# Where norms, state attention and output weights stand in a streaming encoder step on one Trainium2 core

## The chip, the core and the metric

The kernel is one launch on one NeuronCore of a Trainium2 chip. The metric is device time in microseconds, the median of repeated executions, lower is better. TensorE (PE) does the matrix products, VectorE (DVE) and ScalarE (ACT) the elementwise work, GpSimd (POOL) broadcasts and issues part of the DMAs, and SyncE (SP) issues the rest.

## What is computed

One layer of a hybrid encoder over 2048 prompt tokens and 8 x 16 sample tokens, model width 1024, all in float32. Cut to what matters:

```python
u = rms_norm(x, norm_mix) @ w_in             # 21 tiles of 128 columns, split among four mixers
mix = concat(ssd(u), swa(u), shortconv(u), conformer(u))
x = x + mix @ w_out
hf = rms_norm(x, norm_ffn)
x = x + (silu(hf @ w_gate) * (hf @ w_up)) @ w_down      # d_ff = 2816 = 22 tiles
y = rms_norm(x, norm_final)
```

The sample tokens carry their own history: `ssd` starts from a state `h0`, `swa` (attention) also reads a cache of 128 keys and values for each of 8 sequences. The state after the step is an output too.

## The kernel before, in words

Features lie on the partitions, tokens on the free axis. The tokens are cut into five chunks c0 to c4 of 256, 512, 512, 512 (384 of the prompt and the 128 sample tokens) and 384. A float32 product is made as three products of rounded operands: each weight tile (128 x 1024) and each activation tile is split in a high part (a copy on ACT) and a low part (a subtraction on DVE), and `group` (L239 to L241) issues high x high, high x low and low x high. A *unit* is one weight tile against one chunk: 8 slices x 3 matmuls = 24 matmuls into one PSUM bank of the four of pool `pm`.

`load_w` either loads a raw weight tile of 512 KB into one of two `fr` buffers and splits it into one of three `w` buffers (L204 on ACT, L184 on DVE), or, where an earlier chunk has stored the split pair in DRAM (`kept`, 1 MB, stored from the POOL queue, L227), loads that pair straight into `w` (L219). `keep(c, n)` stores the even tiles at c1 and the rest at c2. `proj_out` asked for that as well, so that the tiles of `w_out` were loaded raw by c0, by c1 and, for four of them, by c2, and split by four loads at c2, eight at c3 and eight at c4.

`weave(units, (tokens, a, b), ...)` sets the order. It runs the units one after the other and spreads each list of side tokens evenly over the unit numbers a to b; a token is one step of a generator up to its next `yield`. Matmuls of a token come behind the last matmul of the unit before it (`issue_after`). The program is then put in one order for each engine when it is built: an instruction stands where its buffers and inputs are expected to be ready, earlier text goes first, and weight loads are pulled ahead (`high_priority`). On the chip each engine and each DMA queue works its list strictly in that order.

The pieces that matter here:

- `norm1` (L334) makes the eight normalised, split input tiles `xn` of a chunk, `norm2` (L866) those of the feed-forward part, `final` (L931) the output. Each begins by spreading a row of 1/rms over the partitions with a few matmuls (L272), and then goes through eight tiles. `norm1` reads its tiles again from DRAM into `nt`, of which there are three buffers that `add_square` also uses for the squares of `proj_out`.
- `proj_out` (L840) loads the residual tile `x2[m]` (L849), adds the PSUM bank to it (L184) and then squares it. There are eight `x2` buffers. The one of unit m is free when `final` of the chunk before has written tile m to DRAM (L939).
- `raw_tiles` gives one of two `raw` buffers to the outputs `a`, `h`, `B`, `C`, `x0`, `x1` of `proj_in`. With the sample chunk c3, the history is loaded into it and the new history stored from it (L398, 12 KB) before it is free again. The buffer of `a0` stays in use until the 31 taps of the conformer convolution are done.
- `mixers` makes the tokens of a chunk: three (two, four) blocks of prompt attention and ssd, the sample's attention and ssd where there is a sample, the conformer convolution, and the ends. `attend_sample` and `load_h0` put the state, keys and values into `act` buffers, of which there are 16; at c3 eight hold `xn` of c3 and eight the feed-forward input of c2 until the last `proj_in` unit of c3 (`z1`) has read them.

The last 896 tokens (c3, c4) go through the feed-forward part together at the end, as two halves of 448 (`quad`, `product`); `drain` adds and squares the result and `final2` norms and stores it.

Of the kernel before, what the change touches and what calls it, by code (L numbers as in the profile page):

```python
# [17 lines left out]
P = 128  # L18
# [100 lines left out]
def stream_step(ctx: ExitStack, tc: tile.TileContext, cfg, x, w_in, w_out, w_gu, w_down, tab, con, dist_p, dist_s,  # L119
# [23 lines left out]
    def mk(pool_, shape, tag, dt=F32, **kw):  # L143
        uid[0] += 1
        return pool_.tile(shape, dt, tag=tag, name=f"{tag}_{uid[0]}", **kw)
# [188 lines left out]
    def norm1(c):  # L334
        T, o = c["T"], c["off"]
        r = spread(c["r1"], T)
        c["xn"] = []
        for k in range(KT):
            if "x" in c:
                xt = c["x"][k]  # L340
            else:
                xt = mk(np_, [P, TM], "nt", bufs=B["nt"])[:, :T]
                sync.dma_start(xt, x[:, k, o:o + T])
            stt(xt, xt, T_("gmix", k), r, ALU.mult, ALU.mult)
            d = mk(ap, [P, 2, TM], "act", F32R)
            split(d, xt, T)
            c["xn"].append(d)
            if k == 3:
                yield
        yield  # L350

# [436 lines left out]
    def mixers(c, early=False):  # L788

        st = []  # L790
        c["mix"] = [None] * 8

        def add(*gens):

            todo = [[g, n] for g, n in gens]
            while any(n for _, n in todo):
                for t in todo:
                    if t[1]:
                        st.append(t[0])
                        t[1] -= 1  # L800

        if c["Ts"]:
            def load_h0():
                c["h0"] = []
                for i in range(2):
                    c["h0"].append(mk(ap, [P, DEC_B // 2, 256], "act"))
                    pool.dma_start(c["h0"][i], h0[:, 4 * i:4 * i + 4])
            add((once(load_h0), 1))
            add((attend_sample(c), 3), (ssd(c, c["Tp"], True), 2))
        short = once(lambda: [mix_tile(c, 4 + t, c["u"][f"y{t}"][:, :c["T"]]) for t in range(2)])  # L810
        if not early:
            add((short, 1))
        convs = [(j, k, min(31, k + 8)) for j in range(2) for k in range(0, 31, 8)]
        nb = c["nt"]
        for b in range(nb):
            add((attend_prompt(c, b), 3), (ssd(c, b * P, False), 2))
            mine = convs[len(convs) * b // nb:len(convs) * (b + 1) // nb] if not early else []
            for j, k0, k1 in mine:
                add((once(lambda j=j, k0=k0, k1=k1: conf_conv(c, j, k0, k1)), 1))
        if early:  # L820
            c["blocks"] = len(st)
            for j, k0, k1 in convs:
                add((once(lambda j=j, k0=k0, k1=k1: conf_conv(c, j, k0, k1)), 1))
            add((short, 1))
        add((end_conf(c), 3), (end_ssd(c), 3))
        add((once(lambda: [mix_tile(c, 2 + g, c["u"][f"q{g}"][:, :c["T"]]) for g in range(2)]), 1))
        return st
# [12 lines left out]
    def proj_out(c):  # L840
        T, o = c["T"], c["off"]
        c["x2"] = []

        def unit(m):
            if m == 0:
                c["ss"] = mk(np_, [P, TM], "ns", bufs=1)[:, :T]
            park = c["i"] >= cfg.nfirst
            x2 = mk(np_, [P, TM], "nt", bufs=B["nt"]) if park else mk(np_, [P, TM], "x2", bufs=8)
            sync.dma_start(x2[:, :T], x[:, m, o:o + T])  # L849
            wh, wl = load_w(w_out[m], [KT, P], len(W_IN_TILES) + m, keep(c, m))  # L850
            ps = mk(pm, [P, 512], "pm")
            group(ps, T, [(wh[:, k], wl[:, k], c["mix"][k]) for k in (4, 5, 2, 3, 0, 1, 6, 7)])
            tt(x2[:, :T], x2[:, :T], ps[:, :T], ALU.add)
            if park:
                pool.dma_start(mid[:, m, o - tail_off:o - tail_off + T], x2[:, :T])
            add_square(c["ss"], x2[:, :T], T, m == 0)
            c["x2"].append(x2)

        return [lambda m=m: unit(m) for m in range(KT)]
# [6 lines left out]
    def norm2(c):  # L866
        T = c["T"]
        r = rstd_of(c["ss"], T, D)
        yield
        r = spread(r, T)  # L870
        c["hf"] = []
        for k in range(KT):
            t = mk(np_, [P, TM], "nt", bufs=B["nt"])[:, :T]
            stt(t, c["x2"][k][:, :T], T_("gffn", k), r, ALU.mult, ALU.mult)
            d = mk(ap, [P, 2, TM], "act", F32R)
            split(d, t, T)
            c["hf"].append(d)
        yield

    def ffn(c):  # L880
# [50 lines left out]
    def final(c):  # L931
        T, o = c["T"], c["off"]
        r = rstd_of(c["ss"], T, D)
        yield
        r = spread(r, T)
        for k in range(KT):
            t = c["x2"][k][:, :T]
            stt(t, t, T_("gfin", k), r, ALU.mult, ALU.mult)
            (sync if c["i"] == last else pool).dma_start(y[:, k, o:o + T], t)  # L939
        yield  # L940


# [31 lines left out]
                j += 1  # L974
        return out

    for t in twice(norm1_stats(chunks[0])) + twice(norm1(chunks[0])):
        run(t)
    c0, c1, c2, c3, c4 = chunks
    units = proj_in(c0, FIRST)  # L980
# [2 lines left out]
    m0 = mixers(c0, True)  # L983
    nb0 = c0["blocks"]

    weave(units, (twice(norm1_stats(c1)) + twice(norm1(c1)), 6, n - 1), (m0[:nb0], 10, 22),
          (m0[nb0:], 18, len(units) - 1))
    for c, nxt, after in ((c0, c1, c2), (c1, c2, c3)):
        i = c["i"]
        weave(proj_out(c), *([(twice(final(chunks[i - 1])), 0, 2), (twice(norm1(nxt)), 0, 3)] if i else []))  # L990
        weave(proj_in(nxt, W_IN_TILES[0 if i else EARLY:]), (twice(norm2(c)), 0, 2))
        units = ffn(c)
        weave(units, (mixers(nxt), 0, int(len(units) * 0.85)),
              (twice(norm1_stats(after)), int(len(units) * 0.3), len(units) // 2))

    weave(proj_out(c2), (twice(final(c1)), 0, 4), (twice(norm1(c3)), 1, 5))
    f = ffn(c2)
    def beside(c, s, units, end):

# [5 lines left out]
                (st[n + 4:n + 9], at["a1"], end - 8), (st[n + 9:], end - 7, end)]  # L1005

    s3 = proj_in(c3, SPREAD)
    units = s3[:3] + merge(s3[3:], f[:26]) + f[26:36]
    weave(units, (twice(norm2(c2)), 0, 2), *beside(c3, s3, units, len(units) - 1), (twice(norm1_stats(c4)), 20, 35))
    s4 = proj_in(c4, SPREAD)  # L1010
    units = proj_out(c3) + f[36:39] + merge(s4, f[39:44]) + f[44:53]
    weave(units, ([stats2(c3)], 8, 9), (twice(norm1(c4)), 8, 11), *beside(c4, s4, units, len(units) - 1))


    N = NB
# [162 lines left out]
    units = []  # L1178
    for j in range(0, cfg.nff, 2):
        units += [lambda j=j: gate2(j), lambda j=j: up2(j)]  # L1180
    weave(units, (twice(final(c2)), 0, 2))
    later.close()
    rp = ctx.enter_context(tc.tile_pool(name="rp", bufs=KT, side="right", reuse_waits="tile"))
    ht = ctx.enter_context(tc.tile_pool(name="ht", bufs=F["ht"], side="right", reuse_waits="tile"))
# [6 lines left out]
    def drain(h, m, ps):  # L1191
# [5 lines left out]
        else:  # L1197
            q = mk(np_, [P, TM], "nt", bufs=B["nt"])[:, :N]
            act.activation(q, v, AF.Square)
            tt(ss[h], ss[h], q, ALU.add)  # L1200

    def operand(j, h):
        if j >= cfg.nff - 2:
# [17 lines left out]
    def final2(h):  # L1221
# [1 line left out]
        v, r, t = (mk(cp, [P, 8], "n8", bufs=9)[:, :nb] for _ in range(3))  # L1223
        pc = mk(px, [P, 512], "px")
        for i, b in enumerate(blk):
            pe.matmul(pc[:, i:i + 1], ss[h][:, b:b + P], ones[:, 0:1], start=True, stop=True)
        newton(v, r, t, pc[:, :nb], D)
        yield
        rb = spread_one([(r[:, i:i + 1], 0, b, P) for i, b in enumerate(blk)])
# [170 lines left out]
```

## Time and profile before

| | |
|---|---|
| median of 3 runs | 2426.2 us (2425.7 to 2428.43) |
| the profiled execution | 2428.43 us |
| its span on the core | 2426.7 us, mean granted clock 0.992 |
| PE busy | 2355.6 us, 97% |
| DVE busy | 1573.4 us, 65% |
| ACT busy | 859.9 us, 35% |
| POOL busy | 149.4 us, 6% |
| DMA | 436.25 MB, mean 180 GB/s |

The span is the time from the first to the last instruction of the profiled execution; the 1.7 us beside it lie outside the instructions. A busy PE is a PE with a matmul in its pipeline. The time of the profiled execution is the highest of the three runs, 2.2 us above the median.

### The profile page before, as it was taken

Reading aid. Unit: us, or ns where it says so; the run is one execution under the profiler, and the core shown is the slowest. Engines: PE = TensorE matmul, PEld = TensorE weight load, DVE = VectorE, ACT = ScalarE, POOL = GpSimd, SP = SyncE. Lnnn points to the kernel's source line nnn. Section 1 sums busy time; section 2 is a strip of 40 time slices with the busy share of each in tenths; the row PEclk is TensorE's granted clock in tenths of the full one; section 3 lists DMA queues with packets and bytes.
Section 4 is the critical chain, followed back from the end, with each engine's and each line's share of the span. In section 5 each row is a group of like instructions: output and inputs, shape, how many; then the busy total and the mean of one; then the engine's idle time right before and its main releaser. Section 6 shows DMA issues by size and latency. Waiting matters only on the chain.

```text
span 2426.7 us, 32445 instructions
## 1 busy us (share of the span) xinstructions
PE 2355.6 (97%) x12443; PEld 2043.0 (84%) x12443; DVE 1573.4 (65%) x2982; ACT 859.9 (35%) x1446; POOL 149.4 (6%) x274
## 2 busy tenths in 40 slices
PE   6999999999999999989999999999999999999997
PEld 6888999888888888877788778988879999999997
DVE  7998998866884445457562564675487667673324
ACT  5544555433333333222211241232244444442221
POOL 0000000000000000001000000000001000000000
PEclk9999999999999999999999999999999999999998
DMA  6546444677555455575544327653733332338653
GB/s 213 204 157 225 154 152 162 209 281 274 183 176 177 169 183 174 202 293 148 191 158 165 140 105 266 211 171 127 265 110 126 122 123 96 125 122 307 214 188 119
DMA packets 134619, 436.25 MB, mean 180 GB/s; under 512 B 13008, under 2 KB 50800, under 8 KB 113728
## 3 DMA queue, kind: packets, MB, share of 16 engines
q1 hardware_dynamic: 115536, 335.06, 41.4%
q0 software_dynamic: 18928, 99.12, 10.6%
q8 instruction: 98, 1.61, 0.3%
q14 instruction: 57, 0.47, 0.1%
HBM read 334.55 MB, written 99.57 MB: 179 GB/s over the span
## 4 chain that ended last, share of the span: by engine, by line
PE 68%; issue 16%; DVE 7%; DMA 6%; ACT 2%; POOL 1%; SPq 0%; DVEq 0%; POOLq 0%; ACTq 0%
PE pm L239 13%; PE pm L240 13%; PE pm L241 13%; PE pm L1114 7%; PE pm L1115 7%; PE pm L1116 7%; DVE mix L187 2%; DVE w L184 2%; DMA nt<-x 2%; PE px L1116 1%; PE px L1115 1%; PE px L1114 1%; DMA fr<-w_in 1%; DMA w<-kept 1%; ACT w L204 1%
## 5 line engine op out<-in xcount | busy, mean ns | idle before, releaser
L239 PE MATMUL pm<-act,w 128*128 128x512 f32 (+2 forms) x2216 | 800.7, 362 | 17.5 <-DMA w<-kept 9.7
L241 PE MATMUL pm<-act,w 128*128 128x512 f32 (+2 forms) x2216 | 794.4, 359 | 4.7 <-DVE w L184 4.7
L240 PE MATMUL pm<-act,w 128*128 128x512 f32 (+2 forms) x2216 | 793.2, 358 | 0.5 <-DVE act L184 0.5
L204 ACT ACTIVATE w<-fr 128x1024 fp32r<-128x1024 f32 (+3 forms) x360 | 372.4, 1035 | 843.5 <-PE pm L241 476.6
L184 DVE TENSOR_TENSOR w<-fr,w 128x1024 fp32r<-128x1024 f32 (+3 forms) x360 | 429.6, 1194 | 274.6 <-ACT w L204 271.9
L239 PEld LDWEIGHTS pm<-act,w 128*128 128x128 f32 x2216 | 417.9, 189 | 83.0 <-issue 13.8
L241 PEld LDWEIGHTS pm<-act,w 128*128 128x128 f32 x2216 | 418.1, 189 | 64.7 <-DVE w L184 6.4
L240 PEld LDWEIGHTS pm<-act,w 128*128 128x128 f32 x2216 | 418.4, 189 | 58.2 <-DVE act L184 1.3
L1114 PE MATMUL pm<-hf,w 128*128 128x448 f32 x616 | 225.4, 366 | 0.9 <-ACT g L1128 0.9
L1115 PE MATMUL pm<-hf,w 128*128 128x448 f32 x616 | 224.8, 365 | 0.0
L1116 PE MATMUL pm<-hf,w 128*128 128x448 f32 x616 | 223.8, 363 | 0.0
L187 DVE SCALAR_TENSOR_TENSOR mix<-raw,tabh,mix 128x384 f32<-128x384 f32 (+3 forms) x360 | 202.2, 592 | 2.3
L239 PE MATMUL pm<-h,w 128*128 128x512 f32 (+1 forms) x528 | 191.2, 363 | 6.0 <-ACT hf L199 3.3
L241 PE MATMUL pm<-h,w 128*128 128x512 f32 (+1 forms) x528 | 187.4, 356 | 0.0
L240 PE MATMUL pm<-h,w 128*128 128x512 f32 (+1 forms) x528 | 187.2, 355 | 0.0
L184 DVE TENSOR_TENSOR x<-x,pm 128x512 f32<-128x512 f32 (+2 forms) x184 | 107.8, 599 | 86.2 <-PE pm L241 70.1
L187 DVE SCALAR_TENSOR_TENSOR ft<-ft,pm 128x512 f32<-128x512 f32 (+1 forms) x132 | 78.5, 594 | 98.9 <-PE pm L241 83.3
L1114 PEld LDWEIGHTS pm<-hf,w 128*128 128x128 f32 x616 | 115.5, 188 | 10.3 <-ACT g L1128 1.2
L1116 PEld LDWEIGHTS pm<-hf,w 128*128 128x128 f32 x616 | 115.7, 188 | 9.4
L1115 PEld LDWEIGHTS pm<-hf,w 128*128 128x128 f32 x616 | 115.7, 188 | 8.3
L239 PEld LDWEIGHTS pm<-h,w 128*128 128x128 f32 x528 | 99.7, 189 | 24.4 <-issue 3.8
L241 PEld LDWEIGHTS pm<-h,w 128*128 128x128 f32 x528 | 99.7, 189 | 15.3
(283 smaller groups left out, 2585.3 us busy)
## 6 DMA issues: line engine op xcount, KB each, us to landing
w<-kept SPq DMA_DIRECT2D x103, 1024.0 KB, 5.3
fr<-w_gu SPq DMA_DIRECT2D x154, 512.0 KB, 3.3
kept<-w POOLq DMA_DIRECT2D x59, 1024.0 KB, 6.4
fr<-w_down SPq DMA_DIRECT2D x84, 512.0 KB, 3.6
fr<-w_in SPq DMA_DIRECT2D x52, 512.0 KB, 4.0
hm<-h POOLq DMA_DIRECT2D x44, 448.0 KB, 4.7
ht<-hm SPq DMA_DIRECT2D x40, 448.0 KB, 4.7
nt<-x SPq DMA_DIRECT2D x56, 256.0 KB, 4.7
```

The costliest lines, as they stand in the source:

```text
L184: return eng.tensor_tensor(out=out, in0=a, in1=b, op=op)
L187: return eng.scalar_tensor_tensor(out=out, in0=a, scalar=s, in1=b, op0=op0, op1=op1)
L204: act.activation(d[:, 0, :n], raw, AF.Copy)
L239: pe.matmul(ps[:, :T], wh, o[:, 0, :T], start=(i == 0), stop=False)
L240: pe.matmul(ps[:, :T], wh, o[:, 1, :T], start=False, stop=False)
L241: mm = pe.matmul(ps[:, :T], wl, o[:, 0, :T], start=False, stop=(i == n - 1))
L1114: pe.matmul(ps[:, :N], wh[:, i], a, start=first and i == 0, stop=False, skip_group_check=True)
L1115: pe.matmul(ps[:, :N], wh[:, i], b, start=False, stop=False, skip_group_check=True)
L1116: mm = pe.matmul(ps[:, :N], wl[:, i], a, start=False, stop=(i == n - 1), skip_group_check=True)
```

## The change

- `w_out` is no longer stored split: `load_w` of `proj_out` gets no key, so each chunk loads the raw tile and splits it. Twenty loads of 1 MB become loads of 512 KB with a split each, and eight stores of 1 MB go.
- `norm1` yields after tiles 1, 3 and 5 (four parts instead of two), `norm2` and `final` after the row and after tiles 1, 3 and 5 (five parts instead of two), and the `weave` calls spread these parts over more units. In `proj_out` of c2, for instance, `final(c1)` has its row of 1/rms spread behind unit 1 instead of unit 2, and the four pairs of tiles behind units 1, 3, 4 and 6; `norm1(c3)` has its pairs behind units 1, 2, 4 and 6 instead of its halves behind units 1 and 3. In `proj_out` of c1, `norm1(c2)` moves from units 0 and 1 to units 1, 2, 4 and 6.
- In the stretch that makes `proj_in` of c3 beside the feed-forward part of c2, the first units were g0, a0, B, C, gate, up, x0, gate, x1, ... and are now g0, a0, B, C, x0, x1, gate, up, dt, gate, ....
- In a chunk whose mixers run early (c3), the loads of the sample's state, its attention and its ssd come behind those of the three prompt blocks instead of ahead of them.
- In the last half, the squares of the last tile are not added to the sum on DVE; `final2` adds the two in PSUM with a second matmul for each block of tokens.
- `final` issues its stores from POOL in every case. It is only called for c0, c1 and c2, for which that was so before.

```diff
@@ norm1 @@
-            if k == 3:
+            if k in (1, 3, 5):
                 yield
@@ mixers @@
-        if c["Ts"]:
-            def load_h0():
+        def load_h0():
...
+        def sample():
             add((once(load_h0), 1))
             add((attend_sample(c), 3), (ssd(c, c["Tp"], True), 2))
+
+        if c["Ts"] and not early:
+            sample()
...
+        if c["Ts"] and early:
+            sample()
         if early:
             c["blocks"] = len(st)
@@ proj_out @@
-            wh, wl = load_w(w_out[m], [KT, P], len(W_IN_TILES) + m, keep(c, m))
+            wh, wl = load_w(w_out[m], [KT, P])
@@ norm2, final @@
+            if k in (1, 3, 5):
+                yield
...
-            (sync if c["i"] == last else pool).dma_start(y[:, k, o:o + T], t)
+            pool.dma_start(y[:, k, o:o + T], t)
@@ the order @@
-    weave(units, (twice(norm1_stats(c1)) + twice(norm1(c1)), 6, n - 1), (m0[:nb0], 10, 22),
+    weave(units, (twice(norm1_stats(c1)) + twice(norm1(c1), 4), 6, n - 1), (m0[:nb0], 10, 22),
...
-        weave(proj_out(c), *([(twice(final(chunks[i - 1])), 0, 2), (twice(norm1(nxt)), 0, 3)] if i else []))
-        weave(proj_in(nxt, W_IN_TILES[0 if i else EARLY:]), (twice(norm2(c)), 0, 2))
+        weave(proj_out(c), *([(twice(final(chunks[i - 1]), 5), 0, 8), (twice(norm1(nxt), 4), 1, 8)] if i else []))
+        weave(proj_in(nxt, W_IN_TILES[0 if i else EARLY:]), (twice(norm2(c), 5), 0, 7))
...
-    weave(proj_out(c2), (twice(final(c1)), 0, 4), (twice(norm1(c3)), 1, 5))
+    weave(proj_out(c2), (twice(final(c1), 5), 0, 8), (twice(norm1(c3), 4), 1, 8))
...
-    units = s3[:3] + merge(s3[3:], f[:26]) + f[26:36]
-    weave(units, (twice(norm2(c2)), 0, 2), *beside(c3, s3, units, len(units) - 1), (twice(norm1_stats(c4)), 20, 35))
+    units = s3[:5] + merge(s3[5:], f[:24]) + f[24:36]
+    weave(units, (twice(norm2(c2), 5), 0, 5), *beside(c3, s3, units, len(units) - 1), (twice(norm1_stats(c4)), 20, 35))
...
-    weave(units, ([stats2(c3)], 8, 9), (twice(norm1(c4)), 8, 11), *beside(c4, s4, units, len(units) - 1))
+    weave(units, ([stats2(c3)], 8, 9), (twice(norm1(c4), 4), 8, 11), *beside(c4, s4, units, len(units) - 1))
...
-    weave(units, (twice(final(c2)), 0, 2))
+    weave(units, (twice(final(c2), 5), 0, 2))
@@ drain, final2 @@
-            tt(ss[h], ss[h], q, ALU.add)
+            if h and m == KT - 1:
+                ss.append(q)
+            else:
+                tt(ss[h], ss[h], q, ALU.add)
...
-            pe.matmul(pc[:, i:i + 1], ss[h][:, b:b + P], ones[:, 0:1], start=True, stop=True)
+            sums = [ss[0]] if not h else ss[1:]
+            for n, sq in enumerate(sums):
+                pe.matmul(pc[:, i:i + 1], sq[:, b:b + P], ones[:, 0:1], start=(n == 0), stop=(n == len(sums) - 1))
```

## Rows read from the trace of the kernel before

**Rows 1.** Busy time of each engine, share of the span, instructions.

```profile
PE 2355.6 (97%) x12443; PEld 2043.0 (84%) x12443; DVE 1573.4 (65%) x2982; ACT 859.9 (35%) x1446; POOL 149.4 (6%) x274
```

**Rows 2.** Waits of PE, whole span: us in total, times, longest.

```profile
PE pm L239 <- DMA w<-kept: 9.7, 5, 3.5
PE pm L239 <- DVE x L184: 6.8, 3, 6.0
PE px L714 <- DMA act<-kc: 4.3, 1, 4.3
```

**Rows 3.** Stretches: us, each engine's busy time, granted clock, DMA share, GB/s.

```profile
163.00:186.00 23.00, 23.00 (x195) 22.94 (x194) 21.03 (x37) 15.09 (x22) 0.00 (x0) 1.00 0.42 144
1019.00:1075.00 56.00, 49.99 (x222) 40.98 (x221) 25.80 (x46) 10.10 (x14) 5.94 (x11) 0.94 0.82 310
1447.00:1491.00 44.00, 44.00 (x194) 36.11 (x193) 11.25 (x17) 5.49 (x8) 3.81 (x7) 1.00 0.73 251
1695.00:1730.00 35.00, 33.73 (x194) 33.35 (x193) 8.78 (x16) 4.58 (x9) 3.24 (x6) 1.00 0.80 284
...
1044.05:1050.30 6.25, 0.25 (x2) 0.00 (x0) 1.34 (x3) 0.01 (x1) 1.20 (x3) 0.82 1.02 410
1050.30:1058.00 7.70, 7.69 (x24) 6.18 (x25) 3.26 (x5) 1.25 (x2) 0.54 (x1) 0.70 1.02 408
...
1347.00:1355.30 8.30, 8.30 (x51) 5.48 (x46) 4.05 (x13) 0.88 (x4) 0.00 (x0) 0.50 0.06 24
...
1116.27:1175.00 58.73, 52.30 (x217) 41.39 (x216) 51.06 (x122) 17.69 (x31) 7.40 (x8) 0.97 0.60 197
```

**Rows 4.** The chain that ended last, in order: start us, us, what.

```profile
1039.87 2.31 DMA y<-x
1042.19 7.25 DMA x<-x
...
1122.86 10.29 DMA o_xc_s<-raw
...
1337.31 9.46 DMA act<-kc
...
1731.77 7.52 DMA w<-kept
```

**Rows 5.** Waits of PE from 460 to 515 us.

```profile
PE px L272 <- DVE n L187: 1.0, 1, 1.0
```

**Rows 6.** DMA issues: out<-in queue xcount, KB each, median us to landing.

```profile
w<-kept SPq DMA_DIRECT2D x103, 1024.0 KB, 5.3
fr<-w_out SPq DMA_DIRECT2D x20, 512.0 KB, 3.9
```

**Rows 7.** Groups of instructions: busy us, mean ns, idle before and its releasers.

```profile
L184 DVE TENSOR_TENSOR w<-fr,w 128x1024 fp32r<-128x1024 f32 (+3 forms) x360 | 429.6, 1194 | 274.6 <-ACT w L204 271.9 <-DMA w<-kept 1.3
L204 ACT ACTIVATE w<-fr 128x1024 fp32r<-128x1024 f32 (+3 forms) x360 | 372.4, 1035 | 843.5 <-PE pm L241 476.6 <-PE pm L1116 115.1 <-PE px L1116 66.3
```

**Rows 8.** SP's queue in order: start us, us, issues of `norm1(c3)`.

```profile
1054.38 3.12 SPq L343 DMA_DIRECT2D nt<-x  x3
```

**Rows 9.** DVE in order: the last tiles of `norm1(c3)`.

```profile
1078.68 1.89 DVE L184 TENSOR_TENSOR act<-nt,act 128x512 fp32r<-128x512 f32 x3
```

**Rows 10.** ACT in order: PSUM to `raw` for B and for x1.

```profile
1096.59 0.47 ACT L382 ACTIVATE raw<-pm 128x384 f32<-128x384 f32 x1
...
1133.25 0.49 ACT L382 ACTIVATE raw<-pm 128x384 f32<-128x384 f32 x1 [3.88 <-DMA o_xc_s<-raw]
```

**Rows 11.** Waits of PE from 1690 to 1760 us.

```profile
PE pm L239 <- DMA w<-kept: 4.8, 2, 3.5
```

**Rows 12.** All engines in order, the sums of squares at the end.

```profile
2399.50 0.95 PE L1226 MATMUL px<-con,x 128*128 128x1 f32 x8
...
2411.60 1.36 DVE L184 TENSOR_TENSOR x<-x,nt 128x448 f32<-128x448 f32 x2 [0.17 <-ACT nt L1199]
2413.01 1.51 PE L1226 MATMUL px<-con,x 128*128 128x1 f32 x8 [4.09 <-DVE x L184]
```

More of the change, by code (lines that the diff above doesn't have):

```diff
@@ L800, in add @@
                         t[1] -= 1
-        if c["Ts"]:
-            def load_h0():
[L804 to L807, printed above, removed]
+        def load_h0():
+            c["h0"] = []
+            for i in range(2):
+                c["h0"].append(mk(ap, [P, DEC_B // 2, 256], "act"))
+                pool.dma_start(c["h0"][i], h0[:, 4 * i:4 * i + 4])
+        def sample():
             add((once(load_h0), 1))
             add((attend_sample(c), 3), (ssd(c, c["Tp"], True), 2))
+        if c["Ts"] and not early:
+            sample()
         short = once(lambda: [mix_tile(c, 4 + t, c["u"][f"y{t}"][:, :c["T"]]) for t in range(2)])
@@ L938, in final @@
             stt(t, t, T_("gfin", k), r, ALU.mult, ALU.mult)
-            (sync if c["i"] == last else pool).dma_start(y[:, k, o:o + T], t)
+            pool.dma_start(y[:, k, o:o + T], t)
+            if k in (1, 3, 5):
+                yield
         yield
@@ L975, in merge @@
         return out
-    for t in twice(norm1_stats(chunks[0])) + twice(norm1(chunks[0])):
+    for t in twice(norm1_stats(chunks[0])) + twice(norm1(chunks[0]), 4):
         run(t)
```

## The prediction, made before the changed kernel was run

> **What bounds the kernel now.** I read the page's busy times first: PE is busy 97% of a span of 2426.7 us and no other engine over 65% [rows 1]. So what counts is what makes PE wait or run slowly. I take its time for one unit from the stretch of `proj_out` of c3, where it never waits: 44.00 us for 194 matmuls [rows 3], 0.227 us each, 5.44 us for the 24 of a unit of 512 tokens. A long run of units at this pace has nothing to give. The table of PE's waits then names the places outside it: stored weights that land late (9.7 us in 5 waits), a residual added late on DVE (6.0 us at once), and keys that land late (4.3 us) [rows 2]. Last I read the stretches around these waits, since a wait also costs what follows it: behind the residual's wait the granted clock averages 0.70 for 7.70 us, in which PE does 24 matmuls, and behind the keys' wait it is 0.50 (1.2 GHz) for 8.30 us [rows 3].
>
> **The residual in `proj_out` of c2.** Unit 4 needs the PSUM bank of unit 0, so the residual tile of unit 0, so its `x2` buffer, which is free when `final(c1)` has written tile 0. The chain shows that order: store 2.31 us from 1039.87, load 7.25 us from 1042.19 [rows 4], then PE goes on at 1050.3. From the store's start to there are 10.5 us; for the spread and the first tile ahead of it I put 2 us (an estimate: eight small matmuls, 0.95 us in rows 12, one DVE instruction and the issue), 12.5 us in all. In that time PE does unit 3 alone, and waits 6.0 us [rows 2]; the unit after takes 7.70 instead of 5.44 us [rows 3], 2.2 more. The change spreads behind unit 1, a unit earlier: 12.5 us then stand against units 2 and 3, 10.9 us, and two spreads of some 0.9 us. I leave 0.5 us of wait and no slow stretch behind it: **-7.7 us**. The bounds are -8.2 (no wait left) and 0 (the transfers stay as late for another reason, a rival below). In the same stretch four stores and four halves of loads go, 6.3 of its some 17 MB (310 GB/s over 56 us [rows 3]), which should shorten the 7.25 us; I don't count that.
>
> **`proj_out` of c1.** Here `final(c0)` was spread behind unit 1 already. PE waits 1.0 us for the last step of its 1/rms on DVE [rows 5], which stood behind half of `norm1(c2)`; that half now comes after it. **-1.0 us**, bounds -1.5 and +3: `norm1(c2)` starts one unit later and can be late for `proj_in`.
>
> **Weights of `w_out`.** Twenty splits cost 20 x 1.194 = 23.9 us of DVE and 20 x 1.035 = 20.7 us of ACT [rows 7]. They lie beside PE: DVE was busy 11.25 of 44.00 us in c3's stretch and 8.78 of 35.00 in c4's, and eight splits add 9.6 to each; c2 adds four, 4.8, to 25.80 of 56.00 [rows 3]. If that cover were gone, a tile would need 3.9 us to land [rows 6] and 2.2 to be split, with two raw buffers some 3.1 us a unit, under the 4.2 us of a unit of 384 tokens. c0 shows it: 195 matmuls of 256 tokens with eight raw tiles in 23.00 us, and PE busy throughout [rows 3]. What is gained: in c4's stretch eight loads of 1 MB fill the DMA engines (share 0.80, 284 GB/s [rows 3]), and PE waits there and just behind it 4.8 us, 3.5 at once [rows 11]. The other 1.3 us are a `w_out` tile's and go. The 3.5 us are those of a feed-forward tile that stays stored and takes 7.52 us [rows 4] after short units; less traffic may give 0.6 of it. **-1.9 us**, bounds -4.8 and 0. The eight stores no longer stand in POOL's queue, between the stores of `final`; I count nothing for that.
>
> **The stretch of c3's `proj_in`.** From 1116 to 1175 us PE does 217 matmuls, 49.3 us at 0.227, in 58.7: 9.4 us are lost, with DVE busy 51 of 58.7 [rows 3]. B, C, x0 and x1 share one `raw` buffer while a0 has the other. Each holds it until its 12 KB of history are stored, 10.29 us at the worst [rows 4]; from B's eviction to x1's are 36.7 us, 12.2 a step [rows 10]. Before, feed-forward units stood between them; now PE finishes C, x0 and x1 in the 16 us behind B, and x1's bank is held until 36.7 us behind B. Gate, up and dt fill 16 more, and the next unit, gate1, would come at 32.6 and find one of the four banks still taken: about 4 us, if the bank's turn is in order, nothing if not. The work of DVE in the stretch is the same, `norm2(c2)` only thinner. I take **+2.5 us**, bounds -6 and +14 (rivals). `norm2`'s last pair is due behind unit 4, and the first gate that reads it is unit 6.
>
> **The sample behind the prompt.** State, keys and values land in buffers that z1's matmuls release. The keys are third in POOL's queue and take 9.46 us [rows 4]; PE's list has their first use some 5 us after the issue, hence 4.3 us of wait [rows 2]. Moved behind the prompt's attention, the sample still needs the buffers of z1, the same transfers still go out then, and PE's list still puts the use where the keys are expected. What moves ahead is the prompt's attention, into units where DVE is free. **0 us** in the likeliest case, bounds -8.4 (the wait, and at most half of the 8.30 us at 0.50) and +4. POOL's broadcasts for the prompt come ahead of these loads, long before z1.
>
> **The rest: 0.** `norm1(c1)`, `norm2` and `final` elsewhere do the same instructions in thinner portions, units ahead of their use (`norm2(c0)`: last pair behind unit 5, first reader unit 10), or, for `norm1(c4)`, at the same units but for one pair; bounds -1.5 and +1.5. At the end a DVE addition goes: the two additions take 1.36 us [rows 12], so 0.7 us. The matmuls of the sums double from 8 to 16. Eight take 0.95 us earlier, at full clock, and 1.51 us here [rows 12]: +0.8 to +1.5, part of which starts earlier on the sum that is ready. Net +0.1 to +0.8, taken as 0.3 and lost in the rounding. The Trainium skill (TensorE: Matmul & The Clock Gate, in the part "Wait — 56ns, not 53.3ns?") puts the start-to-start floor of small matmuls at about 25 ns, by which eight more would cost 0.2 us and the edit gain 0.5; the row is 0.1 to 0.19 us for each with its weight load, so the measured row decides here.
>
> **Sum:** -7.7 -1.0 -1.9 +2.5 +0.3 = -7.8 us. The profiled execution would go from 2428.43 (2426.7 and 1.7 around it) to 2420.6; against the median of 2426.2, which is 2.2 lower, that is **2418.4 us**.
>
> **Rivals.** (1) *The sample's wait goes too.* For it: the prompt's tokens no longer stand behind it, and fewer things crowd z1's end. Against it: the loads' release is unchanged. -6.5 more (4.3 and about half of the bound behind it): 2412. (2) *A new wait on `xn`.* In `proj_out` of c1 and c2, `norm1`'s loads share three `nt` buffers with the squares, and all now stand behind unit 1's square. Eight tiles took from 1054.4 to 1080.6 [rows 8, 9], 26 us. In c2 they could start at about 1045 and would end at 1071; `proj_in` reaches its last slice at about 1071.7. Half a microsecond of slack: if each of the four pairs is 1.5 us later, PE waits some 5 us here and 1 in c1. That gives 2424, no measurable change. (3) *Slower, through `raw`.* If on DVE the first copies into `raw` for x0 and x1 stand ahead of the splits of up0 and gate1, DVE holds those splits until the buffer is free, 24.4 and 36.7 us behind B [rows 10], 2.4 us more for the split itself. It decides when the order puts a copy ahead of a split: up0 would start 5 us late, gate1 some more, and DVE, the fullest engine there [rows 3], has 10 us less for what follows. +14 instead of +2.5: 2430, and with rival 2 besides 2435. (4) *The earlier spread does nothing*, because `x2` loads stand behind something else on SP: -7.7 falls away, 2426.
>
> **Chances.** The likeliest 0.42 (own range 2413 to 2422; of it 0.36 below 2421.3), rival 1 0.20, rival 2 0.19, rival 3 0.12, rival 4 0.07. A measurement of this kernel tells 0.2%, 4.9 us, from no change. Faster: 0.36 + 0.20 + 0.11 of rivals 2, 3 and 4 at their mild ends = 0.67. Slower: 0.11, most of rival 3. Same: the rest, 0.22. The range takes rival 1 and its bound at the low end and rivals 2 and 4 and part of 3 at the high end: 2405 to 2430.
>
> **What would show it.** The wait of `L239 <- DVE x L184` near 1050 us under 1 us and full clock there; no `w<-kept` wait inside c4's `proj_out`; evictions of B, C, x0, x1 still some 12 us apart; a wait for the keys still near 4 us; `L1226` x16 at the end. A long wait of the first `proj_in` unit on `act`, or of an early gate or up on its split, would make the number wrong upwards; a missing wait on the keys downwards.

## The result, and the profile after

The changed kernel's median is 2419.9 us (2410.5 to 2426.1, 18 executions), that of the kernel before, run beside it, 2433.1 us (2425.1 to 2442.2, 18 executions). The ratio is 0.9942, 95% interval 0.9927 to 0.9956: 14 us less (11 to 18). The forecast was 7.8 us less. That the forecast time of 2418.4 us is so close to the measured one is luck: the 2426.2 us that it started from lay at the low end of what the kernel before gives.

The two profiled executions differ by less than the medians do: 2424.9 us after against 2428.4 before. The one is at the long end of its kernel's times, the other at the short end of its own. So the comparison below says where time went in this pair; how much of it is the kernel's, the experiments show.

The page's busy times:

```profile
PE 2358.7 (97%) x12451; PEld 2049.9 (85%) x12451; DVE 1597.3 (66%) x3001; ACT 880.8 (36%) x1466; POOL 144.2 (6%) x266
```

The waits of PE over the whole span (us in total, times, longest):

```profile
PE pm L239 <- ACT act L199: 7.4, 4, 3.9
PE pm L240 <- DVE act L184: 7.3, 2, 6.0
...
PE px L714 <- DMA act<-kc: 2.3, 1, 2.3
PE pm L239 <- DMA w<-kept: 1.8, 1, 1.8
```

Against [rows 2], the waits for stored weights fell from 9.7 to 1.8 us, that for keys from 4.3 to 2.3, and the residual's wait of 6.0 is gone. In their place stand two rows for `act`, operands that ScalarE and VectorE write: 14.7 us, where the kernel before had 1.5.

The stretches, with the columns of [rows 3]: `proj_out` of c2, of c3 and of c4, the new wait, and the slow clock behind the keys:

```profile
1019.00:1075.00 56.00, 54.73 (x255) 45.17 (x254) 37.08 (x62) 17.79 (x25) 4.34 (x8) 1.00 0.67 236
1447.00:1491.00 44.00, 44.00 (x194) 36.11 (x193) 18.71 (x23) 11.82 (x15) 4.33 (x8) 1.00 0.57 196
1695.00:1730.00 35.00, 35.00 (x201) 34.42 (x200) 18.81 (x29) 10.97 (x17) 4.33 (x8) 1.00 0.64 203
1112.10:1125.80 13.70, 5.40 (x12) 3.81 (x13) 8.94 (x23) 2.85 (x6) 1.78 (x2) 0.50 0.51 89
1351.00:1361.20 10.20, 10.06 (x55) 6.86 (x56) 5.62 (x18) 1.86 (x7) 0.29 (x1) 0.50 0.15 57
```

In c2's `proj_out` PE does 255 matmuls in the 56 us that held 222, at a granted clock of 1.00, and the DMA engines go from 0.82 and 310 GB/s to 0.67 and 236. VectorE is busy 11.3 us more in that window, and PE's one wait there is short (1.3 us for `act`):

```profile
PE pm L240 <- DVE act L184: 1.3, 1, 1.3
```

At 1112 us it is the other way: 12 matmuls in 13.7 us at 0.50, which is 1.2 GHz.

The DMA issues over the span (KB each, median us to landing), against [rows 6]: 20 loads of a stored 1 MB became 20 raw ones of 0.5 MB, and both kinds land sooner.

```profile
w<-kept SPq DMA_DIRECT2D x83, 1024.0 KB, 4.9
...
fr<-w_out SPq DMA_DIRECT2D x40, 512.0 KB, 3.2
```

What the new wait is, VectorE's instructions in order show (start us, us, instruction; in brackets the idle time before it and who ended it):

```profile
1097.88 0.17 DVE L356 COPY raw<-hx 128x3 f32<-128x3 f32 x1 [3.80 <-DMA o_xc_s<-raw]
...
1108.52 0.75 DVE L187 SCALAR_TENSOR_TENSOR nt<-x,tab,px 128x512 f32<-128x512 f32 x1
1109.17 0.17 DVE L356 COPY raw<-hx 128x3 f32<-128x3 f32 x1
1115.02 0.35 DVE L192 TENSOR_SCALAR xx<-raw,tabh 128x128 f32<-128x128 f32 x1 [5.68 <-DMA raw<-xst]
...
1115.74 0.69 DVE L184 TENSOR_TENSOR act<-nt,act 128x512 fp32r<-128x512 f32 x1
```

ScalarE's in the same stretch, the evictions of B, C, x0 and x1:

```profile
1088.10 0.47 ACT L382 ACTIVATE raw<-pm 128x384 f32<-128x384 f32 x1
...
1097.96 0.49 ACT L382 ACTIVATE raw<-pm 128x384 f32<-128x384 f32 x1 [5.48 <-DMA o_xc_s<-raw]
...
1107.64 0.49 ACT L382 ACTIVATE raw<-pm 128x384 f32<-128x384 f32 x1
...
1120.56 0.49 ACT L382 ACTIVATE raw<-pm 128x384 f32<-128x384 f32 x1 [1.09 <-DMA o_xc_s<-raw]
```

ScalarE frees one PSUM tile into `raw` every 9.7 to 12.9 us, as the chain of stores lets it. A tile of `norm2(c2)` is scaled at 1108.52, but its low half is written only at 1115.74: VectorE stands in between on the convolution of x0, 5.68 us of it idle for the history that loads into `raw`. The last parts of `norm2(c2)`, now due behind units 3 and 4, share VectorE's queue with that chain, and the first gate waits for them.

At the end, the sums of squares (durations min/median/max in ns, first and last start in us); the second row is the eight new matmuls:

```profile
L1241 PE MATMUL px<-con,x x16: 164/301/370, 2394.3 to 2409.9; 128*128 128x1 f32 x16
L1241 PE MATMUL px<-con,nt x8: 352/352/352, 2407.5 to 2410.3; 128*128 128x1 f32 x8
```

PE's wait for VectorE's last addition ahead of them is 3.4 us where it was 4.09 [rows 12].

### The profile page after: what moved, and what is told of

The parts are those of the page before. It is cut to its first block, busy times and chain, and to the rows that moved or that the text cites. A ratio compares the mean times of both kernels' runs of the same rounds, so it can differ in the third digit from the quotient of the medians.

```text
span 2422.8 us, 32494 instructions
## 1 busy us (share of the span) xinstructions
PE 2358.7 (97%) x12451; PEld 2049.9 (85%) x12451; DVE 1597.3 (66%) x3001; ACT 880.8 (36%) x1466; POOL 144.2 (6%) x266
## 4 chain that ended last, share of the span: by engine, by line
PE 81%; issue 6%; DVE 6%; DMA 5%; ACT 2%; POOL 0%; SPq 0%; DVEq 0%; ACTq 0%; POOLq 0%
PE pm L239 17%; PE pm L240 17%; PE pm L241 17%; PE pm L1124 7%; PE pm L1125 7%; PE pm L1126 7%; DVE w L184 2%; PE px L1125 1%; PE px L1124 1%; PE px L1126 1%; DMA nt<-x 1%; ACT w L204 1%; DMA fr<-w_in 1%; DMA o_xc_s<-raw 1%; DVE mix L187 1%
## 5 line engine op out<-in xcount | busy, mean ns | idle before, releaser
L204 ACT ACTIVATE w<-fr 128x1024 fp32r<-128x1024 f32 (+2 forms) x380 | 393.6, 1036 | 893.4 <-PE pm L241 513.0
L184 DVE TENSOR_TENSOR w<-fr,w 128x1024 fp32r<-128x1024 f32 (+2 forms) x380 | 454.3, 1196 | 280.8 <-ACT w L204 279.1
```

The source lines that it names most:

```text
L184: return eng.tensor_tensor(out=out, in0=a, in1=b, op=op)
L204: act.activation(d[:, 0, :n], raw, AF.Copy)
```

## The experiments

Twelve kernels ran in three groups of four, each group beside the kernel before on one chip. The first group is the changed kernel again, raw output weights, the norms and unit orders, and the sample (median of before there 2431.7 us). The second is the spread alone, c3's order, `norm2(c2)` early and keys first (2440.5 us). The third is the spread with raw weights, the bytes, no projection weights kept, and the kernel before again (2434.9 us). Ratios are to the kernel before of the same group, with 95% intervals.

**The changed kernel again.**

> The changed kernel once more, for a second profile of it. Its first profile was 2424.9 us against 2428.4 of the kernel before, a difference of 3.5 us, while the medians of all runs stood 13 us apart (2419.9 and 2433.1). Theory A (the new wait of 2.1, 6.0 and 3.9 us in the stretch of c3's `proj_in`, with 13.7 us at 1.2 GHz behind it, belongs to the order of the work): it stands in this profile again, within 3 us of its size, and the two profiles differ by little. Theory B (it was one execution's chance, from how the transfers of the `raw` copies fell): the wait is gone or under 4 us in all, and the profiled time is near 2412 to 2416 us. Either way the ratio of the medians is 0.992 to 0.996.

0.9957 (0.9939 to 0.9976), median 2421.5, profile 2416.3. The three waits stand again with 2.15, 7.10 and 3.53 us (PE's waits from 1085 to 1130 us), and two other kernels with this order had them too (the norms and orders alone, and keys first):

```profile
PE pm L240 <- DVE act L184: 7.1, 1, 7.1
PE pm L239 <- ACT act L199: 5.7, 2, 3.5
```

So they are the order's (A); yet this profile is 8.6 us shorter than the first one, so the two differ by more than A had it.

**Raw output weights alone.**

```
-            wh, wl = load_w(w_out[m], [KT, P], len(W_IN_TILES) + m, keep(c, m))
+            wh, wl = load_w(w_out[m], [KT, P])
```

> The kernel before with one part of the change alone: the output projection's weights are loaded raw and split each time. Theory A (it takes away c4's `proj_out` wait for kept weights and the slow stretch behind it, and no more): -2 to -6 us, with the wait on kept `w` near 1735 us gone and c2's `proj_out` still with its 6 us wait. Theory B (the gain of the whole change is the 19 MB less of transfers): -10 to -14 us, with the other stretches shorter too. Theory C (the 20 splits more on VectorE and ScalarE cost what the wait gives): -1 to +1 us.

0.9946 (0.9927 to 0.9965), median 2418.6. This one line has the time of the whole change: theory B's number, not that of A (-2 to -6), which stood for the forecast's -1.9. C falls as well. Its window of c2's `proj_out`:

```profile
1019.00:1075.00 56.00, 52.51 (x236) 43.13 (x235) 35.51 (x58) 17.40 (x24) 4.34 (x8) 0.97 0.63 219
```

PE's waits from 1035 to 1180 us:

```profile
PE pm L239 <- DMA w<-kept: 4.5, 3, 2.2
PE pm L239 <- DVE x L184: 3.5, 1, 3.5
```

With the spread where it was before, the residual's wait shrank from 6.0 to 3.5 us.

**The norms and unit orders alone.**

```
-        wh, wl = load_w(w_out[m], [KT, P])
+        wh, wl = load_w(w_out[m], [KT, P], len(W_IN_TILES) + m, keep(c, m))
```

The sample and the last squares are as before too.

> The kernel before with the norms in four and five parts and the unit orders of the change, and nothing else of it (kept output weights, the sample first, the last squares added as before). Theory A (c2's `proj_out` gives 8 us, the stretch of c3's `proj_in` takes 14 and gives 6 back behind it): -3 to +2 us, with the waits of 2 to 6 us for `act` at 1105 to 1125 us in the profile. Theory B (those waits come only where the weights are split again and the sample stands behind, so not here): -8 to -12 us, without them. Theory C (the order does nothing): -0.5 to +0.5 us with c2's wait still there.

1.0034 (1.0017 to 1.0051), 8 us slower than before: no theory had it. The waits of A are there, and stored weights are late in addition (a further 4.7 us at 517 us, in c2's `proj_in`). PE's waits from 1035 to 1180 us:

```profile
PE pm L239 <- ACT act L199: 7.0, 2, 4.8
PE pm L240 <- DVE act L184: 5.0, 1, 5.0
PE pm L239 <- DMA w<-kept: 4.5, 2, 3.0
PE pm L239 <- DVE x L184: 1.5, 1, 1.5
```

**The sample behind the prompt alone.**

```
-        if c["Ts"]:
+        if c["Ts"] and not early:
             ...
+        if c["Ts"] and early:
+            sample()
```

> The kernel before with the sample's attention and scan behind the prompt's blocks, and nothing else. Theory A (the keys' wait near 1350 us falls from 4.3 to about 2.3 us, and other small waits of the region with it): -1 to -5 us. Theory B (the wait only moves, since the keys are issued behind the same release of `act`): -1 to +1 us. Theory C (it is the main gain of the change): -8 to -14 us.

1.0013 (0.9997 to 1.0029): no gain. Its keys' wait is 2.6 us instead of 4.3, but the kernel before, run again, had 3.1. Over all profiles this wait is 2.7 to 5.2 us in the seven with the sample first and 1.9 to 5.1 in the seven with it behind, so the edit can't be seen in it.

**The spread alone.**

```
-    weave(proj_out(c2), (twice(final(c1)), 0, 4), ...
+    weave(proj_out(c2), (twice(final(c1), 5), 0, 8), ...
```

`final` has its five parts elsewhere too. In `proj_out` of c1 they are due over units 0 to 2, which puts the spread behind unit 0, a unit earlier than in the changed kernel.

> The kernel before with `final` alone cut in five parts, due over units 0 to 8 of c2's `proj_out`, and 0 to 2 elsewhere (so that its spread comes one unit earlier); the two norms and every order of units are as before. Theory A (the 6.0 us wait of PE near 1050 us in c2's `proj_out` was the spread standing behind unit 2, with VectorE's chain in front of `norm1(c3)`): -6 to -9 us, and none of the new waits of c3's stretch. Theory B (the wait goes only if `norm1(c3)` is cut too, or moves to its `xn`): -2 to +1 us, with a wait of 3 us or more left in that `proj_out`.

0.9998 (0.9980 to 1.0016). A falls. B has the number and the wait of over 3 us that is left, but not its cause: the residual's wait shrinks to 1.2 us, and behind it come two waits for stored weights, none for `xn`. Its window:

```profile
1019.00:1075.00 56.00, 52.20 (x238) 42.35 (x237) 29.85 (x52) 13.58 (x19) 6.50 (x12) 1.00 0.84 303
```

The loads of stored weights in it, and below them those in the same window of the kernel before:

```profile
w<-kept SPq DMA_DIRECT2D x6, 1024.0 KB, 8.5
w<-kept SPq DMA_DIRECT2D x6, 1024.0 KB, 6.9
```

PE's waits from 1019 to 1095 us:

```profile
PE pm L239 <- DMA w<-kept: 5.7, 2, 4.1
PE pm L239 <- DVE x L184: 1.2, 1, 1.2
```

**The spread with raw output weights** (the two edits above together).

> The kernel before with two edits: the output projection's weights loaded raw and split each time, and `final` alone in five parts (the edit of the run with `final` alone, which was no faster by itself: its 6.0 us wait fell to 1.2 us, and two waits of 1.6 and 4.1 us for kept weights stood behind it). Theory A (the two edits need each other: the early spread only lets PE run into kept weights that are 1 MB each): c2's `proj_out` without any wait over 1.5 us, 3 to 6 us less than with raw weights alone, so 0.991 to 0.994 of before. Theory B (raw weights alone already give all of it): the same as with raw weights alone, 0.9946, within 0.001. Theory C (the parts add up singly): also 0.9946, but with waits of over 3 us left in c2's `proj_out`.

0.9936 (0.9913 to 0.9960), median 2419.1. The time can't be told from that of raw weights alone (0.9946), so A's 3 to 6 us less are not shown; the profile shows A's mechanism. In its window PE never waits for weights or residuals:

```profile
1019.00:1075.00 56.00, 56.00 (x258) 46.13 (x257) 37.79 (x61) 18.09 (x26) 4.35 (x8) 1.00 0.68 239
```

The table below is worked out from the traces: the time from PE's matmul 5760 (all its matmuls, in order of their starts), the first behind unit 1 of c2's `proj_out`, to a later matmul, minus the same time in the first profile of before.

```
matmul  before at   control  spread   norms   raw    spread+raw  changed  changed again
                             alone    alone   alone
 5832    1053.89     -0.1    -6.5    -6.2    -2.7     -7.9        -7.9      -7.9
 5880    1065.38     -0.4    -5.2    -4.9    -3.2     -8.4        -8.4      -8.4
 5928    1076.36     -0.2    +0.9    -0.2    -3.2     -8.4        -8.4      -7.6
 6000    1092.47     -0.5    +0.4    -1.5    -4.3     -4.4        -6.8      -7.6
 6120    1119.93     -0.5    +1.6   +13.9    -4.1     -4.3        +8.5      +8.8
```

The spread alone gains 6.5 us by matmul 5832 and has given back all of it by 5928, at the `proj_out`'s end. With raw weights it keeps 8.4 us, of which 4 go by matmul 6000, 1.9 of them in a wait for the statistics of `norm2(c2)`. The last two columns then lose 15 and 16 us at the waits for `act`.

**The bytes put back.** The split weights are still stored, and in the text each raw load of a weight that is stored is followed by a copy that nothing reads:

```
                 sync.dma_start(pat(raw[:, :n]), src)
+                if key in kept:
+                    uid[0] += 1
+                    sync.dma_start(dp.tile([P, n], F32, ...), kept[key][:, 0])
```

> As the run with raw output weights alone (0.9946 of before), but the transferred bytes are put back: the split weights are still stored, and each raw load that was a load of kept weights before is followed on SP's queue by a copy of 0.5 MB from the kept weights to a place in the chip's memory that nothing reads. So the splits are on the chip, and the transfers are those of before. Theory A (the gain is the bytes: PE waits where the loads of a stretch are more than its DMA rings bring): back to 0.998 to 1.002 of before. Theory B (the gain is that a raw tile lands sooner than a kept one of twice its size, whatever else is on the queue): stays at 0.993 to 0.997. Theory C (a copy inside the memory costs more than a load): slower than before by over 0.3%.

1.0048 (1.0030 to 1.0066): the gain is gone, and more. But the copies did not run where they are written. A copy waits for nothing but the store of its tile, and so the program's order put all twenty ahead: SP issues twelve of them from 474 to 520 us, in c1's `proj_out` and c2's `proj_in`, eight from 1032 to 1093 us, and none in `proj_out` of c3 and c4, for whose loads sixteen of them stand. The first twelve are of the tiles that c1 stores, the other eight of those that c2 stores (durations in ns, first and last start in us):

```profile
L225 SPq DMA_DIRECT2D extra<-kept x20: 470/522/1519, 474.0 to 1093.3; - x20
```

The transfers come to the 436.25 MB of before, but 110.06 MB are written to memory instead of 99.57, and they lie elsewhere. So neither what the saved bytes are worth in all (A) nor the price of a copy (C) can be read from the ratio. The stretches, again against the first profile of before, say more (us; how they are cut stands below):

```
                                      bytes back   stored           raw
2880 to 4320 (c1's proj_out)            +5.3        0.0 to  +5.8    -1.9 to +1.4
5760 to 7680 (c2's proj_out to c3's)   +10.2       -6.4 to  +4.5   -10.1 to -1.8
8640 to 9400 (c4's proj_out)            -4.6       -0.9 to  +7.2    -4.6 to -2.0
```

Where the copies ran, around c2's `proj_out`, the gain is gone, and there B falls; in c4's, where none ran, it stands. In c2's `proj_out` every transfer takes longer than with raw weights alone (there `y<-x` took 4.5 us, `x<-x` 4.5, `fr<-w_out` 3.3), as the DMA issues of the window from 1019 to 1075 us show:

```profile
fr<-w_out SPq DMA_DIRECT2D x6, 512.0 KB, 5.5
extra<-kept SPq DMA_DIRECT2D x5, 512.0 KB, 6.7
y<-x POOLq DMA_DIRECT2D x8, 256.0 KB, 9.5
x<-x SPq DMA_DIRECT2D x8, 256.0 KB, 6.5
```

The residual's wait, among PE's waits from 1035 to 1180 us:

```profile
PE pm L242 <- DVE x L184: 9.4, 1, 9.4
```

**c3's order as before**, in the changed kernel:

```
-    units = s3[:5] + merge(s3[5:], f[:24]) + f[24:36]
-    weave(units, (twice(norm2(c2), 5), 0, 5), ...
+    units = s3[:3] + merge(s3[3:], f[:26]) + f[26:36]
+    weave(units, (twice(norm2(c2), 5), 0, 2), ...
```

> The changed kernel with the c3 stretch's unit order of before (three units of c3 ahead of the feed-forward's) and `norm2(c2)` due behind units 0 to 1. Theory A (the new waits for `act` at 1110 to 1122 us come from the last tiles of `norm2(c2)` standing behind copies that wait for the `raw` chain of units 3 and 4): those waits gone, the waits of 1146 to 1171 us back (about 6 us), net -4 to -9 us against the changed kernel, so 0.988 to 0.991 of before. Theory B (the waits come from the five parts or from the splits of the output weights): they stay, and the time is that of the changed kernel within 2 us.

0.9919 (0.9892 to 0.9946), median 2419.9. The waits for `act` are gone, and those for stored weights back, as A has it. Waits of PE from 1085 to 1180 us, below them those of the kernel before:

```profile
PE pm L239 <- DMA w<-kept: 5.3, 3, 3.0
PE pm L241 <- DVE w L184: 1.7, 1, 1.7
...
PE pm L239 <- DMA w<-kept: 4.9, 3, 2.9
PE pm L241 <- DVE w L184: 1.5, 1, 1.5
```

The ratio lies just above A's 0.988 to 0.991, and its interval meets that of the changed kernel, so a net gain over the changed kernel is not shown.

**`norm2(c2)` early, the changed unit order kept.**

```
-    weave(units, (twice(norm2(c2), 5), 0, 5), ...
+    weave(units, (twice(norm2(c2), 5), 0, 2), ...
```

> The changed kernel with the five c3 units first, as changed, but all of `norm2(c2)` due behind units 0 and 1. Theory A (the last tiles of `norm2(c2)` are late because they stand behind the `raw` copies): the waits for `act` at 1110 to 1122 us gone, and the waits of 1146 to 1171 us stay away too: -8 to -13 us against the changed kernel, about 0.985 to 0.990 of before. Theory B (the two units more ahead of the feed-forward cost the wait by themselves, since `raw` loads and stores hold the engine): some 6 us or more of waits stay there, and the time is within 4 us of the changed kernel's.

0.9934 (0.9910 to 0.9959), median 2424.0, against 2419.9 for c3's old order in the same group. The waits for `act` are gone, so their cause was that `norm2` came late; but others take their place, and A's -8 to -13 us don't come. B's numbers fit. Waits from 1085 to 1180 us:

```profile
PE pm L239 <- DMA w<-kept: 8.2, 3, 6.0
PE pm L241 <- DVE w L184: 4.4, 2, 3.7
PE pm L239 <- ACT w L204: 2.0, 1, 2.0
```

**Keys first.**

```
-            add((once(load_h0), 1))
-            add((attend_sample(c), 3), (ssd(c, c["Tp"], True), 2))
+            g = attend_sample(c)
+            add((g, 1), (once(load_h0), 1))
+            add((g, 2), (ssd(c, c["Tp"], True), 2))
```

> The changed kernel with the loads of the sample's keys and values issued ahead of the two of its state, all else as changed. Theory A (the keys land late because their issue stands 1.4 us behind the state's two issues and shares the transfer with them): the wait of 2.3 us near 1351 us and the slow clock behind it (10.2 us at 1.2 GHz) shrink or go, -1 to -7 us. Theory B (the release of `act` that all four wait for sets it): the wait stays over 1.5 us, 0 to -1 us.

0.9946 (0.9925 to 0.9967). The wait is 2.0 us instead of 2.3: B. POOL issues the keys as soon as `act` is released (39.8 us idle ahead of it), and that release sets the wait:

```profile
1345.98 0.54 POOL L703 DMA_DIRECT2D act<-kc  x1 [39.82 <-PE pm L241]
```

**No projection weights kept**, with c3's order as before:

```
     def keep(c, n):
-        return c["i"] in (1, 2) and (c["i"] == 2 or n % 2 == 0)
+        return False
```

> The changed kernel with the c3 order of before (the run that had 0.9919), and the input projection's weights not kept either: all 29 tiles of both projections are loaded raw and split in every chunk. Theory A (kept loads of 1 MB are what PE still waits for in the stretches of c3 and c4: 2.9, 1.7, 5.1 and 1.8 us in that run's profile): those waits fall under 1 us each, -3 to -8 us, 0.988 to 0.991 of before. Theory B (the some 50 splits more, about 1.2 us each on VectorE and 1.0 on ScalarE, make VectorE late in the stretches where it is over 75% busy): new waits for `act`, `nt` or `w` from VectorE and ScalarE, 0 to +10 us against that run.

0.9917 (0.9894 to 0.9940), median 2414.0 (2406.6 to 2416.9), profile 2406.6. VectorE rises to 69% and nothing new waits for it, so B falls. The waits for projection weights go, as A has it, but the time against c3's old order does not show A's -3 to -8 us. Waits from 1035 to 1180 us, where only a feed-forward weight that stays stored is late:

```profile
PE pm L239 <- DMA w<-kept: 2.4, 1, 2.4
PE px L265 <- DVE ns L184: 0.7, 1, 0.7
```

This is the lowest median of all. Its ratio is the same as that of c3's old order with stored input weights (0.9919), and its interval touches that of the changed kernel (0.9927 to 0.9956), measured in another group. That it beats the kernel before is shown; that it beats the changed one by some 5 us is likely and not settled.

**The kernel before again.**

> The kernel before, unchanged, for a second profile and to see what two identical kernels give. Its ratio should be 1.000 within 0.002. Theory A (the first profile of before, 2428.4 us, was one of its shorter executions; the medians since are 2432 to 2440): the profile is 2432 to 2442 us, the time more lies in the stretches with kept output weights (c1's and c2's `proj_out`, c3's and c4's), and c2's 6 us wait stands again. Theory B (the added time lies anywhere, as in the stage of c0 too): spread over all stretches.

0.9993 (0.9972 to 1.0014). The profiled execution took 2424.2 us, even less than the first, so A's 2432 to 2442 didn't come, and where the longer executions lose their time is not shown. Its window of c2's `proj_out` is that of the first:

```profile
1019.00:1075.00 56.00, 49.92 (x222) 40.82 (x221) 26.78 (x47) 10.10 (x14) 6.50 (x12) 0.94 0.83 307
```

## Why the prediction was right in its total and wrong in its terms

**Weights of `w_out`: -1.9 predicted, -13 measured (9 to 18).** This is the step that failed. The one line gives 0.9946 alone. In c4's stretch, where the term looked, the waits for stored weights went from 4.8 us to 1.8 and 1.7 in the two profiles, though before's second profile has 2.3 there; most of the gain lies elsewhere. I had looked for waits that name a `w_out` tile and found 1.3 us in c4. In the paragraph on c2 I noted that 6.3 of 17 MB go from a stretch at 310 GB/s, and counted nothing for it, and nothing either for the eight stores that leave POOL's queue. The check I left out is bytes per unit of PE: in c2's `proj_out` eight units need 4 x 1.05 MB of stored loads, 4 x 0.52 of raw loads, 4 x 1.05 of stores, and three transfers of 0.26 MB each for residual, `norm1` and `final`: 16.8 MB, 2.1 MB in each 5.44 us, 386 GB/s. The most that a stretch of [rows 3] showed is 410, at a DMA share of 1.02. So these transfers left little slack; that the lateness of one became that of the next fits this, and is argued. With raw weights the same sum is 10.5 MB, 241 GB/s. (The 236 GB/s in the row of after are not this sum: that window holds over ten units and four loads of other stored weights.) The run with the bytes put back supports it in part: the splits stayed everywhere, the gain went in c2's stretch, into which eight copies fell, and stood in c4's, which got none. It does not show how much of the 13 us the bytes are, since all the copies ran elsewhere than the loads that they stand for. Nor does any run part the bytes of the four stores in c2 from their place in POOL's queue among the stores of `final`.

A rule of the Trainium skill would have spoken for the larger loads (DMA: Bandwidth & Descriptors, in the part on bandwidth measured from HBM to SBUF: batch transfers to 1 MiB and more for at least 75% of the peak). The rows agree per byte, 1 MB in 4.9 us against 0.5 MB in 3.2; but PE waits for a tile, not for a byte, and here the smaller load won.

Where the 13 us lie needs several profiles. I cut each trace at the starts of matmuls 0, 2880, 4320, 5760, 7680 and 10080 and compare the times between cuts with the first profile of before. Means of the five executions with stored output weights (before, control, norms, sample and spread alone) and of seven with raw ones (all others but the one with bytes put back and the one with no projection weights kept):

```
                                     stored   raw    difference
start to matmul 2880 (428 us)         +2.3    +3.1     +0.8
c1's proj_out (2880 to 4320)          +2.2    -1.0     -3.2
c2's proj_out to c3's (5760 to 7680)  -0.3    -4.6     -4.4
c3's proj_out past c4's (to 10080)    +2.1    -3.7     -5.8
```

The sum is -12.6 us; the stretches left out, from 4320 to 5760 and from 10080 to the end, differ by 0.0 and -0.3. In c1 only four stores go, since its loads were raw before; past matmul 7680 no split weight is stored in any of these kernels, and only loads shrink. These kernels differ in other edits too, and one stretch of unchanged code (past matmul 7680) ran from -4.2 to +13.4 us in executions with stored weights, so the split over the stretches is rough.

**The residual in c2's `proj_out`: -7.7 predicted, -8.4 found (-6.8 and -7.6 at matmul 6000).** The mechanism is right: the wait near 1050 us goes with the earlier spread, and the slow clock behind it (1.00 over the window, where it was 0.94) with it. What I missed is the condition: it holds only with raw weights. Alone the spread is worth nothing (0.9998). The raw weights, whose -6.3 MB I set aside, were not an extra to this term but what lets it stand. And raw weights alone take 13 us, as much as the whole: in the changed kernel, what the spread gains is spent by matmul 6120, in c3's stretch.

**c1's `proj_out`: -1.0 predicted, -1.5 and -1.8 found** in the two profiles (matmul 2880 to 4320), where before's second profile is at +0.8. The wait of [rows 5] is gone in both, but with raw weights alone it is gone too, so the order need not be what removed it. With the same orders and stored weights the wait is gone and the stretch is at +5.8, with the 4.7 us for a stored weight in it. The number is right; its cause is not settled.

**The stretch of c3's `proj_in`: +2.5, by another way.** Rival 3 named the place, 15 us were lost there (-6.8 to +8.5 in the table), and the evictions are 9.7 to 12.9 us apart as said. But I had the splits of gate and up behind the `raw` copies; it was `norm2(c2)`'s own tiles, which I had put down as due behind unit 4 with the first reader at unit 6, in time. The run with `norm2(c2)` early shows it. A due unit is a place in a queue, not a time: VectorE's queue stood still there for 5.7 us. Then the waits of before at 1146 to 1171 us don't come, the keys wait 2 us less in this pair, and at c3's `proj_out` the changed kernel is at -4.1 and -3.4 in its two profiles: +2.7 and +4.2 since matmul 6000, near the +2.5 by errors that cancel.

**The sample: 0 predicted.** Alone it gains nothing, 1.0013. The keys' wait is set by the release of `act`, as argued and as the run with keys first shows. **Rival 2** came true in small: a wait of 1.3 us on `act` at 1072 us. **The last squares: +0.3** can't be seen: from matmul 12000 to the end the two profiles are 1.3 and 0.2 us over the first of before, the control 0.4.

Taken alone, raw weights, the orders and the sample give -13, +8 and +3 us (the last within the noise), together -2; the whole gives -10 beside the same executions of before (0.9957). The norms' new order costs with stored weights and costs nothing that can be measured with raw ones.

## What to carry to other kernels

Before you cost an edit by the waits that bear its name, add up the bytes that each unit of the critical engine needs and set them against the highest rate that the trace shows: close to it, halving some of the bytes can be worth far more than their own waits. An order that issues work earlier pays only if the next thing in line can arrive earlier too; try it together with what feeds it. Spreading a producer over more units puts it behind whatever else these units queue on its engine. And before you read an experiment that adds transfers, look at when they were issued: one that waits for nothing need not go out where it is written.

## What was not expected of the hardware

Executions of one program on one chip spread by more than the effects sought: before from 2421.8 to 2440.6 us in the first group and 2429.1 to 2450.4 in the second. The standard deviation was 5.4 us over 27 executions of before in the first group, and 4.0 over the first 18 of the changed kernel. A pair of profiles of two such kernels can't show an effect of a few us; that took stretches compared from a common start, and several profiles.

A stored weight's load of 1 MB took 5.3 us in the median over the span [rows 6], 6.9 in c2's `proj_out`, and 8.5 there when the spread moved forward, at nearly the same DMA share (0.84) as before it (0.82).

In c3's stretch a wait of 2.1 us at 1110 was followed by 13.7 us at 1.2 GHz. The 12 matmuls in them took 0.45 us each instead of 0.227, 2.7 us more; with the three waits, 12.0 us together, that makes the 15 lost there.
